# Down product of a hybrid decoder layer: smaller raw tiles, loads one buffer sooner, and a new order on VectorE

## The chip, the cores and the metric

The kernel runs on one core of one Trainium2 chip. The metric is the time of one execution in microseconds (us) of device time. Five engines work side by side, each through its own list of instructions in order: TensorE (PE in the profile; its weight loads are PEld), VectorE (DVE), ScalarE (ACT), GpSimd (POOL) and SyncE (SP), which here only issues DMAs. An instruction waits for semaphores, and what stands behind it on its engine waits with it.

## The reference, cut to what matters

One layer with 512 tokens and a width of 1024: input projections, retention and sparse attention, an output projection with a layer norm, then a SwiGLU feed-forward net of 2816 hidden units and a second layer norm. The change touches the feed-forward net alone:

```python
gate, up = jnp.split(x @ w_gate_up, 2, axis=-1)
ffn = (jax.nn.silu(gate) * up) @ w_down
return layer_norm(DEEPNORM_ALPHA * x + ffn, ln_ffn_gain, ln_ffn_bias)
```

## The kernel before, in words

**Precision.** Every product of two f32 matrices is made of three matmuls in the format fp32r (`mm3`): high part times high part, high times low, low times high. `split` (L84) makes the parts of a tensor: ACT casts it to the high part (L86). The low part is the source minus the high part, either on DVE (L91), or (where its engine argument is `None`) by a scaled copy on ACT (L88), which writes the negated source, and a DMA with addition that POOL issues (L89). The second matmul of an `mm3` needs the low part of the weights, the first only the high one.

**Gate stage.** 22 tiles of hidden units, one `g_cycle` each, seven groups of 12 matmuls a cycle. The weights come as raw tiles `graw`, DVE forms sums of them (`g_sum`, L815, four instructions), and `g_conv` splits the kinds A, B, C, D. Cycle 2 splits kind C of tile 3, whose low part is `gl3C`.

**Down product.** 11 pairs of hidden tiles, `hu`. Five pairs (`PLAIN`: 0, 1, 2, 3 and 10) are multiplied plainly, column half by column half: first the left half, into four PSUM banks (`d_mm`, `l_step`). The other six pairs form three units (2, 3, 4) and are multiplied in Strassen-like blocks: seven products q, in the order 1, 5, 6, 2, 7, 4, 3, for each unit j. This makes 21 blocks (`w_mm(0)` to `w_mm(20)`), each of 12 matmuls. Block i uses the weights that `w_prep` has split, called p{q}_{j} below: blocks 0 to 2 use p1_2, p1_3, p1_4; 3 to 5 p5_2 to p5_4; 6 to 8 p6; 9 to 11 p2; 12 to 14 p7; 15 to 17 p4; 18 to 20 p3. The split of block i+4 is issued behind block i, since its four buffers for each part (tags `wh`, `wl`) are those of the block that has just been read. Left operands are split by `aprep` into tiles called slot, often with a low part by DMA.

**Raw weights.** All raw weight tiles, `graw` and those of the down product, share three buffers (tag `raw`, 8 KB in each partition), and a new load takes the buffer that was set free first. In order: `draw` 0 and 1 (pairs 0 to 3), `draw` 2 (pair 10 alone, which fills half of a buffer), `r1_2`, `r1_3`, `r1_4` (for p1), `r2a`, `r2b`, `r3a`, `r4_2`, `r4_3`, `r4_4` (for p7), `r5a`, `r5b`, then the right half of the plain pairs. All of them are issued by SP, in this order. `r2a` comes into the buffer of `r1_2`, `r2b` into that of `r1_3`, `r3a` into that of `r1_4`; `r4_3` takes that of `r3a`, which is free after p2_3, and `r4_4` that of `r2b`, free after p2_4.

**Sums on DVE.** `t1_` (L1155) subtracts parts of `r1` into small tiles `tw`; `t2_` (L1165) subtracts `tw` from `r2a` and `r2b` in place; `t4_` (L1169) makes `tw` anew from `r3a`, `r2b` and `r2a`; `t3_` (L1173) works in place on `r4`. `s1_` to `s4_` add and subtract blocks of the hidden tiles. `take` (L1212) and `add_to` (L1215) add finished PSUM banks to the result. The banks X hold products 1, 6 and 7, the banks Y product 5. The small tiles have 12 buffers (tag `t`).

Of the kernel before, what the change touches and what calls it, by code (L numbers as in the profile page):

```python
# [16 lines left out]
S = 512  # L17
# [36 lines left out]
def hybrid_layer_kernel(ctx: ExitStack, tc: tile.TileContext, xT, x, pos, w0, wf, wt, wo,  # L54
# [18 lines left out]
    def tmp(name, dt=F32):  # L73
        return tp.tile([P, 512], dt, tag="t", name=name)
# [732 lines left out]
    def g_sum(n, eng=V, which=slice(0, 4)):  # L807
        if n >= NF:
            return
        g, u = graw[n][:, 0], graw[n][:, 1]  # L810
        if n not in gsum:
            gsum[n] = [tmp(f"gs{n}_{i}") for i in range(4)]
        t = gsum[n]
        for dst, a, b in ((0, u[:, :S], g[:, :S]), (1, u[:, S:], t[0]), (2, u[:, S:], u[:, :S]), (3, g[:, S:], t[1]))[which]:
            eng.tensor_tensor(t[dst], a, b, op=ALU.subtract)  # L815
# [58 lines left out]
    def g_cycle(n, between=None):  # L874
        nxt = n + 1 if FIRST <= n + 1 < NF else None
        g_mm(n, "a", "A", 0, "s2", False)
        if n and not held(n - 1):
            g_end(n - 1)
        if between:
            next(between)  # L880
        gp[n]["c"] = psu(f"gc{n}")[:, :Q]
        g_mm(n, "c", "A", 1, "s1", True)
        t = tmp(f"gt{n}")
        gp[n]["t2"], gp[n]["t7"] = t[:, :Q], t[:, Q:]
        A.copy(gp[n]["t2"], gp[n]["a"])
        if n == 1:
            for m in range(FIRST):
                g_silu1(m)
        if n not in (1, 2):
            g_conv(n + 1, "A")  # L890
        if nxt:
            g_open(nxt)
            g_mm(nxt, "a", "B", 0, "11", True)
        g_mm(n, "a", "C", 0, "s3", False)
        if nxt:
            g_t1(nxt)
            g_mm(nxt, "b", "B", 1, "12", True)
        if held(n - 1):
            g_mm(n - 1, "c", "D", 0, "s4", False)
        if n == 0:  # L900
            g_mm(3, "b", "B", 1, "12", True)
        c = gp[n]["c"]
        if n == NF - 1:
            c = tmp("gc")[:, :Q]
            A.copy(c, gp[n]["c"])
            g_mm(n, "c", "D", 0, "s4", False)
        A.copy(gp[n]["t7"], gp[n]["a"])
        if n == 0:
            for b in (2, 3):
                combine("s4", b)  # L910
                hi("s4", b)
            g_sum(1, V, slice(2, 4))
        if n == 1:
            g_conv(2, "A")
            g_sum(2, V, slice(2, 4))
        V.tensor_tensor(gp[n]["t7"], gp[n]["t7"], c, op=ALU.add)
        if n == 2:
            g_conv(3, "A")
        if between:
            next(between)  # L920
        if n == 2:
            g_end(n - 1)
        if n + 2 >= FIRST:
            g_conv(n + 2, "B")
        if n == 0:
            g_add1(3)
        g_mm(n, "a", "C", 1, "22", False)
        if nxt:
            g_u1(nxt)
        if n > 1:  # L930
            g_sum(n + 2)
        g_conv(n + 1, "C")
        if n == 1:
            g_end(0)
            g_sum(3)
        if n == 0:
            for b in (2, 3):
                lo("s4", b)
            g_sum(2, V, slice(0, 2))
        if n < NF - 1 and not held(n):  # L940
            g_mm(n, "c", "D", 0, "s4", False)
        A.activation(gp[n]["h2"], gp[n]["a"], AF.Silu)
        g_conv(n + 1, "D", V if n else None)
        g_load(n + 4)
# [110 lines left out]
    UNITS = [2, 3, 4]  # L1055
# [11 lines left out]
    def wprep(key, pieces, low=V):  # L1067
        wh = wp.tile([P, 1024], F32R, tag="wh", bufs=4, name=f"dh{key}")
        wl = wp.tile([P, 1024], F32R, tag="wl", bufs=4, name=f"dl{key}")
        n = 1024 // len(pieces)  # L1070
        for i, src in enumerate(pieces):
            hi, lo = (t[:, i * n:i * n + n] for t in (wh, wl))
            if len(src.shape) == 3:
                hi, lo = (t.rearrange("p (k c) -> p k c", c=S) for t in (hi, lo))
            split(low, hi, lo, src)
        dw[key] = wh, wl
# [2 lines left out]

    def d_load(c, g):  # L1080

        pairs = ((0, 1), (2, 3), (10,))[g]
        draw[c, g] = raw_load(f"draw{c}_{g}", [(2 * i, wd[k, :, :, c * S:c * S + S]) for i, k in enumerate(pairs)])

    def conv_w(c, k):
        if k == 10:
            t, i = draw[c, 2] if c == 0 else r5b, 0 if c == 0 else 2
        else:
            t, i = draw[c, k // 2], 2 * (k % 2)
        wprep((c, k), [t[:, i:i + 2].rearrange("p k c -> p (k c)")])  # L1090

    def conv_h(m):
        j = m // 2
# [29 lines left out]
    def pq(t):  # L1123
        return t.rearrange("p (q c) -> p q c", q=2)
# [53 lines left out]
    def odd(t, k):  # L1178
        return t.rearrange("p (q k) c -> p q k c", k=2)[:, :, k]

    prep = {
        1: lambda j: wprep(f"p1_{j}", [odd(r1[j], 0)], None),
        5: lambda j: wprep(f"p5_{j}", [tw[j, 0], tw[j, 1]]),
        6: lambda j: wprep(f"p6_{j}", [flat(b22(j))]),
        2: lambda j: wprep(f"p2_{j}", [flat(b21(j))]),
# [6 lines left out]
    def w_prep(i):  # L1192
        q, j = WORDER[i]
        prep[q](j)
# [52 lines left out]
    g_cycle(NF - 2)  # L1247
    d_load(0, 1)
    g_cycle(NF - 1, prepare_down())
    d_load(0, 2)  # L1250
    g_end(NF - 1)

    def r1_load(j):
        r1[j] = raw_load(f"r1_{j}", [(2 * q, wd[2 * j + q, :, 0]) for q in range(2)])
# [4 lines left out]
    A.activation(idle, idle, AF.Sqrt)  # L1259
    left = [psu(f"dl{b}") for b in range(NB)]  # L1260
    r1_load(2)
    conv_w(0, 2)
    conv_h(2)
    for b in range(3):
        for i in range(2):
            d_mm(left[b], 0, i, b, i == 0, False)
    conv_w(0, 3)
    r1_load(3)
    conv_h(3)
    for i in range(2):  # L1270
        d_mm(left[3], 0, i, 3, i == 0, False)
# [4 lines left out]
    conv_h(10)  # L1276
    t1_(2)
    conv_w(0, 10)
    r1_load(4)
    w_prep(0)  # L1280
    r2a = raw_load("r2a", [(i, wd[4 + i, :, 1, S:]) for i in range(4)])

# [5 lines left out]
    t1_(3)  # L1288
    for j in UNITS:
        aprep(5, j, pq(ts[j]), V)  # L1290
    w_prep(1)
    r2b = raw_load("r2b", [(i, wd[8 + i, :, 1, S:]) for i in range(2)] + [(2 + i, wd[8 + i, :, 1, :S]) for i in range(2)])
    t1_(4)

    l_step(3)
    for j in UNITS:
        s2_(j)
    for j in UNITS:
        aprep(6, j, pq(ts[j]), V)
    t2_(2)  # L1300
    w_prep(2)
    r3a = raw_load("r3a", [(i, wd[4 + i, :, 1, :S]) for i in range(4)])
    t2_(3)
    t2_(4)
# [10 lines left out]
    for i in range(18):  # L1315
        q, j = WORDER[i]
        w_mm(i, home_of[q], q in (1, 5))
        if i == 0:
            for u in UNITS:
                s4_(u)  # L1320
        elif i == 1:
            t4_(2)
            t4_(3)
        elif i == 2:
            for t in range(2):
                take(t, cl, X[t])
        elif i == 3:
            aprep(2, 2, blk(2, 0, 1), None)
            aprep(2, 3, blk(3, 0, 1), None)
        elif i == 4:  # L1330
            aprep(2, 4, blk(4, 0, 1), None)
        elif i == 6:
            t4_(4)
        elif i == 7:
            aprep(7, 2, pq(t3s[2]), None)
            t3_(2)
        elif i == 8:
            for u in (3, 4):
                aprep(7, u, pq(t3s[u]), None)
        elif i == 9:  # L1340
            t3_(3)
        elif i == 10:
            t3_(4)
            for u in UNITS:
                aprep(4, u, blk(u, 1, 1), None)
            gf = big.tile([P, 2, D], F32, tag="s8", name="gbf")
            for k, v in enumerate((lfg, lfb)):
                dma(gf[:, k], row(v, D))
        elif i == 12:
            for u in UNITS:  # L1350
                aprep(3, u, pq(ts[u]), None)
        if i < 17:
            w_prep(i + 4)
        else:
            conv_w(1, 10)
        if i == 3:
            r4_load(2)
        elif i == 7:
            r4_load(3)
            r4_load(4)  # L1360
        elif i == 8:
            r5a = raw_load("r5a", [(n, wd[4 + n, :, 1, S:]) for n in range(4)])
        elif i == 9:
            r5b = raw_load("r5b", [(n, wd[8 + n, :, 1, S:]) for n in range(2)] + [(2, wd[10, :, :, S:])])
        elif i == 10:
            d_load(1, 0)
        elif i == 15:
            d_load(1, 1)
        if i == 5:
            for t in range(2):  # L1370
                take(t, cr, Y[t])
            for t in range(2):
                take(2 + t, cr, Y[t])
        elif i == 8:
            for t in range(2):
                add_to(t, cr, X[t])
        elif i == 14:
            for t in range(2):
                take(2 + t, cl, X[t])
            for t in range(2):  # L1380
                add_to(2 + t, cr, X[t])
        elif i == 16:
            for b in range(2):
                add_to(b, cl, left[b])
                stat(b, 0, cl)
        elif i == 17:
            for b in range(2, NB):
                add_to(b, cl, left[b])
                stat(b, 0, cl)
# [106 lines left out]
```

## Time and profile before

| what | value |
|---|---|
| median of 3 runs | 625.13 us (624.58 to 625.94) |
| the profiled execution, its own time | 625.04 us |
| its span from the first to the last instruction | 623.2 us |
| PE busy | 609.9 us, 98% |
| DVE busy | 511.5 us, 82% |
| ACT busy | 325.2 us, 52% |
| POOL busy | 115.7 us, 19% |
| mean granted TensorE clock | 0.997 of full speed |

The profiled execution stands for the others: its time is 0.09 us from the median. The 1.8 us between its span and its time lie around the instructions. The gate stage runs in the middle of the span up to about 499.8 us, the down product behind it. Times in the rows are us from the first instruction. A row of a timeline gives the start, the duration, the engine, the line, the operation, what is written and read, and the count; in brackets stand the idle time before it and what ended it. A row for several instructions in a row gives their duration together.

### The profile page before, as it was taken

How to read it: one execution, taken by the hardware profiler on the slowest of the kernel's cores; microseconds unless marked ns; L12 is line 12 of the kernel's file. 1: busy time of each engine (PE TensorE's matmuls, PEld its weight loads, DVE VectorE, ACT ScalarE, POOL GpSimd, SP SyncE). 2: the span in 40 equal slices, each digit the busy share in tenths (PEclk: the TensorE clock that was granted, in tenths of full speed). 3: DMA queues.
4: the chain of work that ended last, by engine and by line, in shares of the span. 5: the costliest groups of instructions: out<-in, count | busy, mean ns of one | idle time of the engine just before them, and what ended most of it. 6: DMA issues, size and time to landing. Idle time of an engine off the chain costs nothing.

```text
span 623.2 us, 9845 instructions
## 1 busy us (share of the span) xinstructions
PE 609.9 (98%) x3732; PEld 544.4 (87%) x3732; DVE 511.5 (82%) x950; ACT 325.2 (52%) x577; POOL 115.7 (19%) x119
## 2 busy tenths in 40 slices
PE   9999999999999999999999999999999999899995
PEld 7888888888888778889999999999999988687884
DVE  6798687897879877989998888889898896886956
ACT  5643444334333765877645555555465694548300
POOL 1177332421455000241000000000000021214011
PEclk9999999999999999999999999999999999999998
DMA  8877444788544862695433323231413269689602
GB/s 310 282 227 198 137 116 121 199 179 196 135 102 105 327 262 85 160 223 108 127 105 124 103 103 131 73 136 69 136 69 135 102 159 264 160 198 307 212 35 101
DMA packets 31840, 98.49 MB, mean 158 GB/s; under 512 B 3328, under 2 KB 9024, under 8 KB 26160
## 3 DMA queue, kind: packets, MB, share of 16 engines
q1 hardware_dynamic: 20448, 76.23, 35.5%
q0 software_dynamic: 10608, 20.39, 17.9%
q10 hardware_dynamic: 736, 1.25, 0.6%
q8 instruction: 29, 0.48, 0.3%
q14 instruction: 19, 0.16, 0.1%
HBM read 74.52 MB, written 2.10 MB: 123 GB/s over the span
## 4 chain that ended last, share of the span: by engine, by line
PE 70%; DVE 15%; DMA 6%; ACT 3%; issue 3%; POOL 1%; SPq 0%; POOLq 0%; ACTq 0%; DVEq 0%
PE ga L846 17%; PE gc L846 9%; PE pf L96 5%; PE pf L95 5%; PE pf L94 5%; PE gb L846 4%; DMA r<-in_wd_dram 3%; PE pt L94 3%; PE pt L96 3%; PE pt L95 3%; DVE gs L815 2%; PE mx L96 2%; PE mx L94 2%; PE mx L95 2%; PE dr L94 2%
## 5 line engine op out<-in xcount | busy, mean ns | idle before, releaser
L86 ACT CAST wh<-raw 128x1024 fp32r<-128x1024 f32 x44 | 45.9, 1049 | 44.3 <-issue 18.4
L89 POOL DMA_DIRECT2D slot<-hu x9 | 10.9, 1317 | 230.1 <-ACT slot L88 229.5
L96 PE MATMUL pf<-xh,wl 128*128 128x512 f32 x128 | 50.0, 391 | 0.3 <-DVE wl L91 0.3
L94 PE MATMUL pf<-xh,wh 128*128 128x512 f32 x128 | 50.1, 391 | 0.0
L95 PE MATMUL pf<-xl,wh 128*128 128x512 f32 x128 | 50.0, 391 | 0.0
L91 DVE TENSOR_TENSOR wl<-raw,wh 128x1024 fp32r<-128x1024 f32 x25 | 30.5, 1231 | 16.9 <-ACT wh L86 16.6
L94 PE MATMUL pt<-wh,xh 128*128 128x512 f32 x96 | 39.2, 408 | 0.0
L96 PE MATMUL pt<-wh,xl 128*128 128x512 f32 x96 | 37.6, 392 | 0.0
L95 PE MATMUL pt<-wl,xh 128*128 128x512 f32 x96 | 37.5, 390 | 0.0
L435 POOL TENSOR_TENSOR rs<-ve,half 128x1 f32<-128x1 f32 (+1 forms) x11 | 11.8, 1069 | 103.9 <-DVE ve L434 97.8
L815 DVE TENSOR_TENSOR gs<-graw,gs 128x512 f32<-128x512 f32 x44 | 30.3, 688 | 0.8
L815 DVE TENSOR_TENSOR gs<-graw 128x512 f32<-128x512 f32 x44 | 30.1, 685 | 0.0
L96 PEld LDWEIGHTS pf<-xh,wl 128*128 128x128 f32 x128 | 24.0, 188 | 5.8 <-DVE wl L91 0.7
L95 PEld LDWEIGHTS pf<-xl,wh 128*128 128x128 f32 x128 | 24.1, 188 | 4.6
L94 PEld LDWEIGHTS pf<-xh,wh 128*128 128x128 f32 x128 | 24.1, 188 | 4.6
L397 DVE MAX8 m<-score 128x8 f32<-128x256 f32 (+2 forms) x48 | 26.8, 558 | 1.1
L89 POOL DMA_DIRECT2D wl<-raw x19 | 16.9, 890 | 57.1 <-ACT wl L88 50.3
L398 DVE MATCH_REPLACE8 score<-m,score 128x256 f32<-128x256 f32 (+2 forms) x48 | 26.0, 542 | 0.0
L380 ACT ACTIVATE lg<-lg 128x256 f32<-128x256 f32 (+2 forms) x24 | 10.9, 474 | 24.6 <-PE lg L379 22.4
L96 PEld LDWEIGHTS pt<-wh,xl 128*128 128x128 f32 x96 | 18.0, 188 | 3.9
L95 PEld LDWEIGHTS pt<-wl,xh 128*128 128x128 f32 x96 | 18.1, 189 | 3.1
L94 PEld LDWEIGHTS pt<-wh,xh 128*128 128x128 f32 x96 | 18.1, 189 | 3.1
(1121 smaller groups left out, 2082.5 us busy)
## 6 DMA issues: line engine op xcount, KB each, us to landing
graw<-in_wgu_dram SPq DMA_DIRECT2D x22, 1024.0 KB, 4.8
wl<-raw POOLq DMA_DIRECT2D x19, 512.0 KB, 5.5
raw<-in_wf_dram SPq DMA_DIRECT2D x8, 1024.0 KB, 6.4
raw<-in_wo_dram SPq DMA_DIRECT2D x8, 1024.0 KB, 4.9
raw<-in_wt_dram SPq DMA_DIRECT2D x6, 1024.0 KB, 5.2
r<-in_wd_dram SPq DMA_DIRECT2D x12, 512.0 KB, 5.9
draw<-in_wd_dram SPq DMA_DIRECT2D x9, 512.0 KB, 5.3
w0s<-in_w_dram SPq DMA_DIRECT2D x8, 320.0 KB, 5.1
```

Source lines behind the costliest of these rows:

```text
L86: A.copy(hi, src)
L89: nc.gpsimd.dma_start(lo.bitcast(F32), src, accum_op=ALU.add)
L91: eng_lo.tensor_tensor(lo, src, hi.bitcast(F32), op=ALU.subtract)
L94: T.matmul(acc, lhsT=lh, rhs=rh, start=first, stop=False, **kw)
L95: T.matmul(acc, lhsT=lh, rhs=rl, start=False, stop=False, **kw)
L96: T.matmul(acc, lhsT=ll, rhs=rh, start=False, stop=last, **kw)
L380: A.activation(lp[:, :n], lp[:, :n], AF.Relu)
L397: V.max(m8, a)
L398: V.match_replace(out=a, in_to_replace=m8, in_values=a, imm_value=TAKEN)
L435: G.tensor_tensor(r[:, :n], e[:, :n], half[:, :n], op=ALU.pow)
L815: eng.tensor_tensor(t[dst], a, b, op=ALU.subtract)
L846: T.matmul(gp[n][acc], lhsT=a[:, i * S + k * P:i * S + k * P + P], rhs=parts[q][:, b, k], start=first and j == 0, stop=j == 11, skip_group ...
```

## The change

- Raw weights of pair 10, left half: no longer a half-filled tile of tag `raw`, but two tiles `d10` of tag `t`, loaded by two DMAs on SP between the loads of `r1_2` and `r1_3`; their split is done in two pieces. So `r1_2`, `r1_3`, `r1_4` each come into the buffer that was one place earlier in the row of loads, and their loads stand earlier in the program.
- p1_4: the low part is made on DVE instead of by DMA with addition.
- `t1_(4)` stands ahead of p1_3 and of the load of `r2b`. p1_4 stands behind the first two of the three splits of product 6's left operand and ahead of `t2_(2)`.
- The four additions out of the banks Y stand two behind block 7 and two behind block 9, instead of all behind block 5. `t3_(2)` stands behind block 8 instead of block 7.
- Gate stage, cycle 2: the sums of tile 4 are formed behind the split of kind C of tile 3, not ahead of it.

```diff
-        if n > 1:
+        if n > 2:
             g_sum(n + 2)
         g_conv(n + 1, "C")
         if n == 1:
             g_end(0)
-            g_sum(3)
+        if n in (1, 2):
+            g_sum(n + 2)
...
-        pairs = ((0, 1), (2, 3), (10,))[g]
+        pairs = ((0, 1), (2, 3))[g]
...
-        if k == 10:
-            t, i = draw[c, 2] if c == 0 else r5b, 0 if c == 0 else 2
+        if k == 10 and c == 0:
+            wprep((c, k), d10)
         else:
-            t, i = draw[c, k // 2], 2 * (k % 2)
-        wprep((c, k), [t[:, i:i + 2].rearrange("p k c -> p (k c)")])
+            t, i = (r5b, 2) if k == 10 else (draw[c, k // 2], 2 * (k % 2))
+            wprep((c, k), [t[:, i:i + 2].rearrange("p k c -> p (k c)")])
...
-        1: lambda j: wprep(f"p1_{j}", [odd(r1[j], 0)], None),
+        1: lambda j: wprep(f"p1_{j}", [odd(r1[j], 0)], None if j < 4 else V),
...
-    d_load(0, 2)
     g_end(NF - 1)
...
     r1_load(2)
+    d10 = [tmp(f"d10_{i}") for i in range(2)]
+    for i in range(2):
+        dma(d10[i], wd[10, :, i, :S])
+    r1_load(3)
     conv_w(0, 2)
...
     conv_w(0, 3)
-    r1_load(3)
+    r1_load(4)
...
     conv_w(0, 10)
-    r1_load(4)
     w_prep(0)
...
+    t1_(4)
     w_prep(1)
     r2b = raw_load("r2b", [(i, wd[8 + i, :, 1, S:]) for i in range(2)] + [(2 + i, wd[8 + i, :, 1, :S]) for i in range(2)])
-    t1_(4)
...
-    for j in UNITS:
+    for j in UNITS[:2]:
         aprep(6, j, pq(ts[j]), V)
+    w_prep(2)
+    aprep(6, 4, pq(ts[4]), V)
     t2_(2)
-    w_prep(2)
...
         elif i == 7:
             aprep(7, 2, pq(t3s[2]), None)
+        elif i == 8:
             t3_(2)
-        elif i == 8:
...
-        if i == 5:
+        if i == 7:
             for t in range(2):
                 take(t, cr, Y[t])
+        elif i == 9:
             for t in range(2):
                 take(2 + t, cr, Y[t])
```

## Rows read from the trace of the kernel before

**Rows 1.** Who waited for whom, PE alone, over the whole span: engine, tile and line, what it waited for, then us in total, times, the longest.

```profile
PE dx L95 <- DMA dlp<-r: 2.9, 1, 2.9
...
PE dx L95 <- DVE dlp L91: 0.6, 1, 0.6
PE ga L846 <- DVE gl3C L91: 0.5, 1, 0.5
```

**Rows 2.** The chain of waits, in order of time, at a place in the gate stage where nothing waits: start, duration, and one group of 12 matmuls.

```profile
391.96 1.44 PE ga L846 x12
```

**Rows 3.** The timeline of PE, single matmuls: in cycle 3 of the gate stage the first two matmuls of kind C of tile 3 and the first of the next group; in the down product the first matmul of block 0, of block 2 with its second and the first of block 3, and of block 14 with its second and the first of block 15.

```profile
314.72 0.28 PE L846 MATMUL ga<-parts,gh3C 128*128 128x256 f32 x1
315.50 0.38 PE L846 MATMUL ga<-parts,gl3C 128*128 128x256 f32 x1 [0.50 <-DVE gl3C L91]
...
316.91 0.28 PE L846 MATMUL gb<-part,gh4B 128*128 128x256 f32 x1
...
527.02 0.39 PE L94 MATMUL dx<-dhp,slot 128*128 128x512 f32 x1
...
532.46 0.39 PE L94 MATMUL dx<-dhp,slot 128*128 128x512 f32 x1
535.74 0.50 PE L95 MATMUL dx<-dlp,slot 128*128 128x512 f32 x1 [2.89 <-DMA dlp<-r]
...
538.37 0.39 PE L94 MATMUL dy<-dhp,slot 128*128 128x512 f32 x1
...
568.29 0.39 PE L94 MATMUL dx<-dhp,slot 128*128 128x512 f32 x1
569.29 0.50 PE L95 MATMUL dx<-dlp,slot 128*128 128x512 f32 x1 [0.62 <-DVE dlp L91]
...
571.93 0.39 PE L94 MATMUL dl<-dhp,slot 128*128 128x512 f32 x1
```

**Rows 4.** The timeline of DVE in cycles 2 and 3 of the gate stage: the low parts of kind B of tile 4, of kind C of tile 3 and, a cycle on, of kind C of tile 4.

```profile
311.02 1.29 DVE L91 TENSOR_TENSOR gl4B<-graw,gh4B 128x512 fp32r<-128x512 f32 x2
...
314.76 1.29 DVE L91 TENSOR_TENSOR gl3C<-gs,gh3C 128x512 fp32r<-128x512 f32 x2
...
323.32 1.28 DVE L91 TENSOR_TENSOR gl4C<-gs,gh4C 128x512 fp32r<-128x512 f32 x2
```

**Rows 5.** The timeline of SP, which issues the loads: r1_2, r1_3, r1_4, r2a, r2b, then r4_3 and r4_4.

```profile
499.72 0.81 SPq L80 DMA_DIRECT2D r<-in_wd_dram  x2
...
506.39 0.80 SPq L80 DMA_DIRECT2D r<-in_wd_dram  x2
...
513.38 1.02 SPq L80 DMA_DIRECT2D r<-in_wd_dram  x2
...
523.51 1.75 SPq L80 DMA_DIRECT2D r2a<-in_wd_dram  x4
...
526.13 1.75 SPq L80 DMA_DIRECT2D r2b<-in_wd_dram  x4
...
554.38 1.19 SPq L80 DMA_DIRECT2D r<-in_wd_dram  x2
...
556.65 1.48 SPq L80 DMA_DIRECT2D r<-in_wd_dram  x2
```

**Rows 6.** The timeline of POOL: its issues of the DMAs with addition that make the low parts of p1_2, p1_3 and p1_4.

```profile
513.20 1.19 POOL L89 DMA_DIRECT2D dlp<-r  x1 [2.54 <-ACT dlp L88]
518.69 1.19 POOL L89 DMA_DIRECT2D dlp<-r  x1 [4.29 <-ACT dlp L88]
527.95 1.19 POOL L89 DMA_DIRECT2D dlp<-r  x1 [8.08 <-ACT dlp L88]
```

**Rows 7.** Who waited for whom, SP alone, between 520 and 537 us, when it issues r2a, r2b and r3a: what they waited for, us in total, times, the longest.

```profile
SPq L80 <- DMA dlp<-r: 17.5, 3, 9.0
```

**Rows 8.** The DMA queues: of POOL (q0) between 519 and 524 us, and of SP (q1) between 526 and 531 us: packets, MB, share of the 16 engines' time.

```profile
q0 software_dynamic: 412, 0.80, 87.2%
...
q1 hardware_dynamic: 791, 1.43, 91.9%
```

**Rows 9.** The timeline of DVE in the down product: the second instruction of t1_(4); t2_(4); the low part of p5_2; those of p6_2 and p6_3; the four additions out of the banks Y; t3_(3), the low part of p7_3, and t3_(4).

```profile
522.54 0.69 DVE L1155 TENSOR_TENSOR tw<-r 128x512 f32<-128x512 f32 x1 [2.03 <-DMA r<-in_wd_dram]
...
529.99 1.29 DVE L1165 TENSOR_TENSOR r2b<-r2b,tw 128x512 f32<-128x512 f32 x2 [0.64 <-DMA r2b<-in_wd_dram]
...
533.01 1.28 DVE L91 TENSOR_TENSOR dlp<-tw,dhp 128x512 fp32r<-128x512 f32 x2
...
545.00 2.36 DVE L91 TENSOR_TENSOR dlp<-r2a,dhp 128x1024 fp32r<-128x1024 f32 x2
...
549.54 2.48 DVE L1212 SCALAR_TENSOR_TENSOR x<-x,dy 128x512 f32<-128x512 f32 x4
...
561.46 1.23 DVE L1173 TENSOR_TENSOR r<-r 128x1024 f32<-128x1024 f32 x1 [2.31 <-DMA r<-in_wd_dram]
563.93 1.23 DVE L91 TENSOR_TENSOR dlp<-r,dhp 128x1024 fp32r<-128x1024 f32 x1 [1.24 <-ACT dhp L86]
565.55 1.23 DVE L1173 TENSOR_TENSOR r<-r 128x1024 f32<-128x1024 f32 x1 [0.40 <-DMA r<-in_wd_dram]
```

**Rows 10.** The timeline of ACT in the down product: the high part of p5_3, which waits for block 0, and the high part of p7_3, which waits for t3_(3).

```profile
529.99 1.14 ACT L86 CAST dhp<-tw 128x512 fp32r<-128x512 f32 x2 [1.30 <-PE dx L96]
...
562.84 1.05 ACT L86 CAST dhp<-r 128x1024 fp32r<-128x1024 f32 x1 [6.14 <-DVE r L1173]
```

## The prediction

> **What bounds the kernel now.** I read the page first: PE is busy for 98% of the span, so little but PE's own waits can be won. Then who waited for whom, PE alone, over the whole span: three waits matter, 2.9, 0.6 and 0.5 us [rows 1]. Then the timeline of PE at these places, since a wait costs more than its idle time: the matmuls behind it also run late. A group of 12 takes 1.44 us in the gate stage [rows 2]; the one of tile 3, kind C, takes 316.91 - 314.72 = 2.19, so 0.75 is lost. A block of the down product takes (532.46 - 527.02) / 2 = 2.72; block 2 takes 538.37 - 532.46 = 5.91 and loses 3.19; block 14 takes 571.93 - 568.29 = 3.64 and loses 0.92 [rows 3]. That is 4.86 us in all, 0.8% of the time. Last I read the timelines of the engines that feed these places. Behind the last block PE goes on without a wait, and the chain from its last matmul to the end stays as it is; what PE gains there, the time gains.
>
> **Gate tile 3.** PE is held by the first half of gl3C, which DVE starts at 314.76, behind four sums of tile 4 [rows 4]. The change puts the sums behind it. The low part of kind B of tile 4 starts at 311.02 and lasts 1.29, so gl3C's first half is there at 312.31 + 0.7 = 313.0, and PE's second matmul wants it at 314.72 + 1.44/12 = 314.84. Gain: 0.75. The four sums end 1.2 us later; next to be late would be gl4C: its first half is there at 323.32 + 0.68 = 324.0 [rows 4], and PE, by then 0.75 earlier, wants it seven groups later, at 314.84 + 7 x 1.44 = 324.9. So moving the sums costs nothing. All times below are in the frame of the old trace, without this 0.75.
>
> **Loads and p1_4.** Block 2 waits for the DMA with addition of p1_4 [rows 1, 3]. It was issued at 527.95 [rows 6], because p1_4 stood behind t1_(4), which waited for r1_4 until 522.54 [rows 9]; r1_4's load was issued only at 513.38, when pair 10 had left its buffer [rows 5]. Now r1_2 comes into the buffer that pair 10 had, r1_3 is issued where r1_2 was (499.72) and r1_4 where r1_3 was (506.39) [rows 5]. With the 9.2 us that r1_4 takes now (513.38 to 522.54, at the longest) it lands by 515.6. The high part of p1_4 then waits for its buffer, which is free when l_step(3) has run. This ends one step of 24 matmuls, 5.44 us, ahead of 527.02, at 521.6; a cast begins 0.25 after the next group's first matmul (529.99 against block 1's start at 529.74) [rows 3, 10], so at 521.8. The low part follows 1.09 later (562.84 to 563.93) and lasts 1.23 [rows 9, 10]: ready at 524.2, wanted at 532.69. Gain: 3.19, with 8 us to spare. What else these instructions cost: DVE gets one low part more and ACT loses a scaled copy, both while DVE would wait for r1_4 or r2b. Behind DVE's new wait stand a split of product 6 (wanted at block 8) and t2_(2), which waits for r2a anyway. POOL loses an issue. On SP two DMAs replace one and stand ahead of r1_3; SP has nothing else to do there until 499.7. The small tiles come from a pool of 12, whose oldest are gate sums read long before. If a tile of the last gate cycle had to be waited for (some 502 us), r1_3 would land 2.3 later and still in time. The second piece of pair 10's split costs ACT and DVE under 0.1 us each. All this I cost at nothing.
>
> **What is late next: r2b.** r2a, r2b and r3a wait for the additions of p1_2, p1_3 and p1_4 to land [rows 7]. r3a now only needs p1_4's DVE instruction and goes out right behind r2b, at 526.13 + 1.75 = 527.9 instead of past 535.74 [rows 3, 5]. At the 0.311 MB/us that SP's queue moved here (1.43 MB in 5 us at 92%) [rows 8] the 2.1 MB of both take 6.7 us, some 534, and t4_ wants r3a at 537.2. r2b still waits for p1_3's addition, issued by POOL at 518.69, which now lands by 526.1, 7.4 us on [rows 5, 6]. If that stays, t2_(4) starts at 529.99 and p5_2's low part at 533.01 as today [rows 9]. From there DVE runs without a gap, 0.60 for each instruction on 512 columns and 1.14 for 1024 (2.48 for four and 2.36 for two, less the overlap) [rows 9]: p5_2, three of s4_, p5_3, four of t4_, p5_4 and two additions make 15 x 0.60 = 9.0, so p6_2's low part is ready at 542.0 + 1.2 = 543.2. Block 6 wants it with its second matmul, at 527.02 + 6 x 2.72 + 2.72/12 = 543.57. Blocks 3 to 5 have 0.5 to 1.7 to spare, so the margin is 0.3 at block 6: I cost it at nothing. How long p1_3's addition takes now is not shown. Nearest rows: its own 7.4 us, 7.8 for p1_4's (527.95 to 535.74) and 10.3 for p1_2's (513.20 to 523.51, when r2a goes out) [rows 3, 5, 6]. Up to 7.7 it costs nothing, and less gains nothing, since no block waits for it; at 10.3 r2b is 2.9 late and block 6 waits 2.6. I take its own.
>
> **What is late after that: block 14.** Its wait in the old trace ends a chain through r4_4: load issued at 556.65, t3_(4) at 565.55 [rows 5, 9]. Both loads now go out earlier, as the four additions no longer stand ahead of p2_3 and p2_4 on DVE. p2_3's cast follows block 6 (546.31), so r4_3 goes out at 546.31 + 1.09 + 1.22 = 548.6; p2_4's follows block 7 (549.03), so r4_4 goes out at 551.3. With today's time from issue to t3_ (7.1 and 8.9) [rows 5, 9] they are there at 555.7 and 560.2. But the two pairs of additions now stand in this very chain. On DVE, one after another: p2_4's low part starts at 549.03 + 1.09 = 550.12; + 1.14 and the additions of Y + 1.20 gives t3_(2) at 552.46. A t3_ and its low part take 1.38 to the cast (561.46 to 562.84), 1.09 to the low part and 1.14: 3.61 [rows 9, 10]. So the additions out of X start at 556.07, t3_(3) at 557.27, the second additions of Y at 560.88, t3_(4) at 562.08. Both loads are in time by 1.5 us or more. p7_4's low part is ready at 562.08 + 1.38 + 1.09 + 1.22 = 565.77, and block 14 wants it at 527.02 + 14 x 2.72 + 0.23 = 565.33. So a wait of 0.44 stays, between a bound of 0 and, were the loads late, more (below), and with the 0.15 by which the rest of such a block is late (571.93 - 569.29 for 11 matmuls, against 2.49) the block loses 0.59. Gain: 0.92 - 0.59 = 0.33. Blocks 12 and 13 want p7_2 and p7_3 at 559.89 and 562.61 and get them at 556.1 and 561.0. What follows (p4, p3, the right half) is tied to these blocks and moves with them.
>
> **The sum.** 0.75 + 3.19 + 0.33 = 4.27. Against the profiled execution's 625.04 that gives 620.8; the median of the runs stands 0.09 higher, so 620.9.
>
> **The rivals.**
> - **No wait is left in block 14.** All 4.86 are won: 620.3. For it: 0.44 us is little at the end of a chain of 16 us. Against it: each term is a measured row, and DVE can't pull anything forward, as it takes its list in order.
> - **r2b comes late.** p1_2's addition took 10.3 us with r1_4's 1.05 MB beside it, 3.4 us of work at 0.311 MB/us; without that, r2a goes out at some 520. So r2a travels beside p1_3's addition, whose 0.52 MB need 2.9 us (0.80 MB in 5 us at 87% is 0.183 MB/us) [rows 8]. If both end together, 6.3 us behind the end of POOL's issue at 519.9, the last byte is there at 526.2, before it is reported. I price that at 1.0 later than now: block 6 waits 0.7 and is 0.15 slower, 621.7. Against it: r1_4's 1.05 MB leave this same stretch. At the bound of 10.3 it is 623.6.
>   The Trainium skill (DMA: Bandwidth & Descriptors, Queues, rings and completion order) says that each DMA engine takes turns between its queues packet by packet. The trace agrees that they share: POOL's queue took 87% of the engines' time in a stretch in which SP's r1_4 was still landing [rows 8, 9]. By that rule this rival, 621.7, would be the forecast.
> - **The loads don't move.** If r1_2 got no earlier buffer, r1_4 would still land at 522.5. Then p1_4's cast and low part on DVE would follow t1_(4) and the splits, done by some 528, still ahead of 532.69: some 621.
> - **Slower: r4_3 late.** Its load now starts beside the DMAs with addition of product 7. t3_(3) wants it at 557.27, 8.7 us after its issue; each us beyond delays p7_3 and, DVE being in order, p7_4 and block 14 by one. At 13 us the whole gain is spent, from 14.2 the kernel is slower by over 0.2%, say 627. For it: two more waiting instructions behind each t3_ than now. Against it: 7.1 us at most today [rows 5, 9].
>
> **How the numbers follow.** A measurement of this kernel tells 0.2%, 1.25 us, from no change. Chances: forecast 0.56, no wait in block 14 0.12, r2b late 0.17 (0.03 of it within 0.2%), loads don't move 0.05, r4_3 late 0.10 (0.04 within, 0.06 slower). So faster 0.87, same 0.07, slower 0.06. The range runs from 619.8, the best case less the 0.55 by which the lowest run lies below the median, to 623.6, r2b at its bound; it leaves out r4_3 late and little else.
>
> **What would show it.** In the new profile: no wait at gl3C; none for a DMA in block 2; r1_4 issued near 505.6 and r3a right behind r2b; in block 14 a wait of about 0.4 for DVE, with t3_(4) started straight behind the additions and not by a DMA. A wait in blocks 3 to 6 would make the r2b step wrong; t3_(3) or t3_(4) released by a DMA, the r4 step.

## The result, and the profile after

The changed kernel takes 620.76 us in the median of four runs (620.34 to 621.16), against 625.54 of the kernel before (624.58 to 626.98) beside it: ratio 0.9922, 95% interval 0.9900 to 0.9943. Forecast were 620.9 and a range of 619.8 to 623.6. The profiled execution is the slowest of the four, 621.16 us with a span of 619.4; it lies 3.88 below the one before, where the sum had 4.27.

Who waited for whom, PE alone, the changed kernel, the two of its five rows that lie in the feed-forward net:

```profile
PE dx L95 <- DVE dlp L91: 0.2, 1, 0.2
PE gc L846 <- DVE gt L916: 0.2, 1, 0.2
```

The wait for the DMA of p1_4 and that for gl3C [rows 1] are gone. The wait of block 14 is down from 0.6 to 0.2. One is new: the last group of cycle 3 of the gate stage (`gc`) waits for an addition on DVE (L916). The other three rows (1.2, 0.4 and 0.2 us) belong to stages ahead of the gate.

The timeline of PE, the changed kernel: kind C of tile 3, the waiting group, and the first matmul of tile 4's kind A; blocks 0, 2 (two matmuls) and 3; block 14 with its second matmul, block 15, and block 18:

```profile
314.33 0.28 PE L846 MATMUL ga<-parts,gh3C 128*128 128x256 f32 x1
...
318.97 0.38 PE L846 MATMUL gc<-parts,gh3D 128*128 128x256 f32 x1 [0.16 <-DVE gt L916]
...
320.50 0.28 PE L846 MATMUL ga<-parts,gh4A 128*128 128x256 f32 x1
...
526.28 0.39 PE L94 MATMUL dx<-dhp,slot 128*128 128x512 f32 x1
...
531.72 0.39 PE L94 MATMUL dx<-dhp,slot 128*128 128x512 f32 x1
531.95 0.39 PE L95 MATMUL dx<-dlp,slot 128*128 128x512 f32 x1
...
534.44 0.39 PE L94 MATMUL dy<-dhp,slot 128*128 128x512 f32 x1
...
564.36 0.39 PE L94 MATMUL dx<-dhp,slot 128*128 128x512 f32 x1
564.99 0.50 PE L95 MATMUL dx<-dlp,slot 128*128 128x512 f32 x1 [0.23 <-DVE dlp L91]
...
567.62 0.39 PE L94 MATMUL dl<-dhp,slot 128*128 128x512 f32 x1
...
575.78 0.39 PE L94 MATMUL dr<-dhp,slot 128*128 128x512 f32 x1
```

Against [rows 3]: block 2 takes 534.44 - 531.72 = 2.72, the undisturbed time, where it took 5.91. Block 14 takes 567.62 - 564.36 = 3.26, where it took 3.64; its second matmul starts 0.40 late. Blocks 0 to 17 take 575.78 - 526.28 = 49.50.

The kernel before, two matmuls that stand in no group: the first of tile 4's kind A and the first of block 18.

```profile
321.23 0.28 PE L846 MATMUL ga<-parts,gh4A 128*128 128x256 f32 x1
...
580.09 0.39 PE L94 MATMUL dr<-dhp,slot 128*128 128x512 f32 x1
```

So blocks 0 to 17 took 580.09 - 527.02 = 53.07 [rows 3]: 3.57 are won there. The four gate groups from kind C of tile 3 to tile 4 took 321.23 - 314.72 = 6.51 and now take 320.50 - 314.33 = 6.17: 0.34. Undisturbed they are 4 x 1.44 = 5.76.

The timeline of SP, the changed kernel: r1_2, r1_3, r1_4, r2a, r2b, r3a, r4_3, r4_4:

```profile
492.62 0.81 SPq L80 DMA_DIRECT2D r<-in_wd_dram  x2
...
498.98 0.81 SPq L80 DMA_DIRECT2D r<-in_wd_dram  x2
...
505.65 0.81 SPq L80 DMA_DIRECT2D r<-in_wd_dram  x2
...
519.74 2.83 SPq L80 DMA_DIRECT2D r2a<-in_wd_dram  x4
...
524.02 1.75 SPq L80 DMA_DIRECT2D r2b<-in_wd_dram  x4
525.88 1.79 SPq L80 DMA_DIRECT2D r3a<-in_wd_dram  x4
...
547.87 1.20 SPq L80 DMA_DIRECT2D r<-in_wd_dram  x2
550.58 1.40 SPq L80 DMA_DIRECT2D r<-in_wd_dram  x2
```

Each load of r1 stands one place earlier than in [rows 5], r3a goes out right behind r2b, and r4_3 and r4_4 go out 6.5 and 6.1 us sooner. r2b too goes out sooner, by 2.1, of which 0.74 is the earlier start of the down product.

Three stretches of PE tell the parts of the change apart better than whole runs do: **gate**, from the first matmul of kind C of tile 3 to that of kind A of tile 4; **blocks**, from the first of block 0 to the first of block 18; **end**, from the first matmul into the last bank (`dc`) to the end of the span. What lies between them is the same in every kernel here (205.8 and 32.8 us). What lies ahead of the gate is not: kind C of tile 3 starts between 313.5 and 315.6 us, in kernels that don't differ up to there. All from the profiled executions; the medians are of whole runs, with that of the kernel before measured beside them:

| kernel | median | before | gate | blocks | end |
|---|---|---|---|---|---|
| before | 625.54 | | 6.51 | 53.07 | 10.3 |
| changed | 620.76 | 625.54 | 6.17 | 49.50 | 10.8 |
| e1 gate order alone | 625.50 | 624.71 | 6.17 | 53.54 | 10.4 |
| e2 changed, p1_4 by DMA | 622.04 | 624.71 | 6.16 | 50.41 | 10.8 |
| e3 changed, loads as before | 621.37 | 624.71 | 6.16 | 50.27 | 10.4 |
| e4 both of these undone | 625.13 | 624.71 | 6.18 | 53.72 | 10.4 |
| e5 additions as before | 622.71 | 626.49 | 6.16 | 50.94 | 10.8 |
| e6 second additions later | 620.55 | 626.49 | 6.18 | 48.96 | 10.8 |
| e7 changed, one DMA less | 620.58 | 626.49 | 6.17 | 49.50 | 10.3 |
| e8 before, one DMA more | 626.48 | 626.49 | 6.51 | 56.79 | 10.7 |
| e0 changed again | 620.83 | 627.00 | 6.16 | 49.48 | 10.8 |
| e9 three edits | 620.20 | 627.00 | 5.76 | 49.12 | 10.4 |
| e10 changed, third time | 621.01 | 627.38 | 6.17 | 49.50 | 10.8 |
| e11 three edits again | 619.97 | 627.38 | 5.76 | 49.20 | 10.3 |

The changed kernel repeats its stretches to 0.02; the kernel before spreads from 622.16 to 629.76 in 61 runs, the changed one from 620.34 to 621.78 in 14. The spread goes with TensorE's granted clock. Among the 59 runs of the kernel before that were measured beside the experiments, the 32 with a mean clock of 0.994 of full speed or less took 624.78 to 629.76, the 13 with 0.997 or more 622.16 to 625.65; the 14 of the changed kernel lie at 0.996 to 0.998. Where the clock falls is shown under e4.

### The profile page after: what moved, and what is told of

It is laid out like the page before. It is cut to its first block, busy times and chain, and to the rows that moved or that the text cites. A ratio compares the mean times of both kernels' runs of the same rounds, so it can differ in the third digit from the quotient of the medians.

```text
span 619.4 us, 9844 instructions
## 1 busy us (share of the span) xinstructions
PE 609.4 (98%) x3732; PEld 544.7 (88%) x3732; DVE 512.3 (83%) x952; ACT 324.4 (52%) x577; POOL 114.1 (18%) x118
## 4 chain that ended last, share of the span: by engine, by line
PE 73%; DVE 15%; ACT 4%; issue 4%; POOL 1%; DMA 1%; ACTq 0%; POOLq 0%; DVEq 0%
PE ga L846 17%; PE gc L846 9%; PE pf L96 5%; PE pf L95 5%; PE pf L94 5%; PE gb L846 4%; PE dl L95 2%; PE dl L94 2%; PE dl L96 2%; PE pt L94 2%; PE pt L96 2%; PE pt L95 2%; DVE gs L815 2%; PE dr L96 2%; PE dr L95 2%
```

## The experiments

**e1: the gate order alone.** The first hunk of the diff, on the kernel before.

> The kernel before with nothing but the new order in cycle 2 of the gate stage. By the prediction's step the second matmul of kind C of tile 3 finds gl3C ready, PE has no wait there, the group takes 1.44 us instead of 2.19, and block 0 of the down product starts 0.75 earlier, at 526.3: 0.75 us less than before, ratio 0.9988. Rival: the sums, now 1.2 us later, make kind C of tile 4 late, and the wait moves there: no change.

Whole runs don't settle it: ratio 0.9997, interval 0.9978 to 1.0016. The stretch does: 6.17, so 0.34 is won, neither 0.75 nor nothing. Its timeline of DVE in cycle 3, low part of kind A of tile 4 and the addition behind it:

```profile
316.99 1.29 DVE L91 TENSOR_TENSOR gl4A<-gs,gh4A 128x512 fp32r<-128x512 f32 x2
318.19 0.41 DVE L916 TENSOR_TENSOR gt<-gt,gc 128x256 f32<-128x256 f32 x1
```

L916 reads the bank `gc`, into which the last group of the cycle goes on adding. It ends at 318.60, and PE starts that group at 318.66. Undisturbed, three groups behind kind C, it would be 314.03 + 3 x 1.44 = 318.35. The wait moved there, not to tile 4's kind C.

**e2: p1_4's low part by DMA, all else as changed.**

```diff
-        1: lambda j: wprep(f"p1_{j}", [odd(r1[j], 0)], None if j < 4 else V),
+        1: lambda j: wprep(f"p1_{j}", [odd(r1[j], 0)], None),
```

> The changed kernel, but the low part of p1_4 is again made by the DMA with addition. Theory: the earlier loads alone carry the step. The cast follows l_step(3) at some 521, POOL issues at some 523.5, and with the 6 to 7.8 us that such additions took it lands at 529.5 to 531.3, ahead of 532.0 when block 2 wants it: no wait in block 2, time as the changed kernel, 620.8. Rival: DVE's low part is what counts: block 2 waits 1 us or more for the DMA, or r3a, which then waits for the addition, makes block 5 wait: 621.8 or more.

622.04. The theory held for block 2, which doesn't wait, and failed for the time. Block 5 waits; DVE and PE show why (second subtraction from r2b; second matmul of block 5):

```profile
530.80 0.69 DVE L1166 TENSOR_TENSOR r2b<-r2b,tw 128x512 f32<-128x512 f32 x1 [2.71 <-DMA r2b<-in_wd_dram]
```

```profile
540.58 0.50 PE L95 MATMUL dy<-dlp,slot 128*128 128x512 f32 x1 [0.35 <-DVE dlp L91]
```

The addition of p1_4 now runs beside r2b's load. In the changed kernel the same two instructions follow each other and wait for nothing, the second at some 527.9:

```profile
527.33 1.29 DVE L1166 TENSOR_TENSOR r2b<-r2b,tw 128x512 f32<-128x512 f32 x2
```

So the second is 2.9 us later in e2. The rival was right that DVE's low part counts, but through r2b, not through block 2 or r3a.

**e3: the loads as before, p1_4's low part on DVE.** `draw` 2 again a raw tile, `d10` gone, each `r1_load` at its old place.

> The changed kernel with the loads as before (pair 10 in a raw tile), the low part of p1_4 still on DVE. Theory, as the prediction's rival of loads that don't move: r1_4 lands at some 521.8, p1_4 is ready at some 527, 5 us ahead of block 2, and the margin at block 6 goes to 0 to 0.3: 620.5 to 621.2. Rival: the loads are what counts, and what stands behind p1_4 on DVE (t2_, p5_2, p5_4) comes late for blocks 3 to 6: 622 to 623.

621.37, 0.17 above the theory's band. Block 2 doesn't wait. Block 5 does, again behind r2b:

```profile
530.26 1.29 DVE L1166 TENSOR_TENSOR r2b<-r2b,tw 128x512 f32<-128x512 f32 x2 [0.48 <-DMA r2b<-in_wd_dram]
```

```profile
540.64 0.50 PE L95 MATMUL dy<-dlp,slot 128*128 128x512 f32 x1 [0.28 <-DVE dlp L91]
```

**e4: both undone.** e3 with e2's edit.

> The changed kernel with the loads as before and the low part of p1_4 by the DMA with addition, so without both halves of that step. Theory: the wait in block 2 comes back, 2.0 to 2.9 us long, since the addition is issued at 526.6 to 527.2 and takes 7 to 7.8: 623 to 623.9. Rival: the order of the splits alone (p1_4 ahead of one split of product 6) brings it in time: below 621.5.

The wait in block 2 is back (PE, block 2's second matmul):

```profile
535.73 0.50 PE L95 MATMUL dx<-dlp,slot 128*128 128x512 f32 x1 [2.31 <-DMA dlp<-r]
```

It is 0.58 shorter than before, and block 14 loses 0.37 less, and yet the blocks take 53.72, 0.65 more than before. The 1.6 between are the clock. PE behind this wait, the kernel before, then e4, then e8, which stands further down (the stretch; its length, busy time and matmuls; the granted clock as a share of full speed; share of the DMA engines, GB/s):

```profile
537.00:540.00 3.00, 3.00 (x15) 1.00 0.93 322
```

```profile
537.00:540.00 3.00, 3.00 (x8) 0.50 0.94 315
```

```profile
536.00:539.00 3.00, 3.00 (x8) 0.50 0.80 270
```

In e4 and e8 the granted clock fell behind the wait to 0.50, the lower of its two levels (1.2 GHz), and then rose again. Some eight matmuls stand 0.43 apart instead of 0.23, so 1.6 us go there. In the profiles of the kernel before and of e1, waits of 2.89 and 2.40 us left the clock at 1.00; e4's was 2.31, e8's 2.92. So the length of the wait alone does not decide it, and what does is not shown. In no other profile here does the clock fall in the blocks.

The median, 625.13, lies 1.2 above what was expected, and the expectation had no term for the clock. That this is the cause is likely, not shown: the profiled execution is the slowest of twelve (626.25), and the others have no trace. With e2 and e3: either half takes the wait out of block 2 (3.3 and 3.5 us of blocks, some 1.6 of them the clock in e4's profile), and only both keep r2b clear (0.9 and 0.8 more).

**e5: the additions and `t3_(2)` back at their places.**

> The changed kernel with the four additions out of the banks Y behind block 5 and t3_(2) behind block 7, as before. Theory: moving them only exchanged one limit for another. r4_3 goes out some 2 us later and r4_4 1.5 us later than in the changed kernel, t3_(4) starts at 560.6 to 562 (561.25 there) and is again released by the DMA of r4_4; block 14 waits 0 to 1.1 us: 620.3 to 621.7, the same within what can be told. Rival: the additions set when the loads start, and all of their 2.4 us come back at block 14: 622.5 or more.

622.71: as the rival said in size. The profiled execution is the second fastest of seven (621.74), and its timeline shows the theory's mechanism, and one more. DVE, t3_(3) and t3_(4); then PE, blocks 14 and 15:

```profile
557.09 1.23 DVE L1174 TENSOR_TENSOR r<-r 128x1024 f32<-128x1024 f32 x1 [3.15 <-DMA r<-in_wd_dram]
...
561.13 1.23 DVE L1174 TENSOR_TENSOR r<-r 128x1024 f32<-128x1024 f32 x1 [0.35 <-DMA r<-in_wd_dram]
```

```profile
564.90 0.50 PE L95 MATMUL dx<-dlp,slot 128*128 128x512 f32 x1 [0.76 <-DVE dlp L91]
...
568.54 0.50 PE L96 MATMUL dl<-dhp,slot 128*128 128x512 f32 x1 [0.40 <-DMA slot<-hu]
```

Both t3_ wait for their loads again, and block 15 waits for the addition of product 4's left operand. So moving the additions and `t3_(2)` is worth 1.44 us of the blocks in this profile (50.94 - 49.50), though it leaves a wait of its own. What the slower runs lose beyond that is in no trace, and the two moves were not tried one by one.

**e6: the second pair of additions behind block 11.**

```diff
-        elif i == 9:
+        elif i == 11:
             for t in range(2):
                 take(2 + t, cr, Y[t])
```

> The changed kernel with its second pair of additions out of Y behind block 11 instead of block 9. Theory: the wait left in block 14 is DVE's list, in order, in which this pair stands. Without it t3_(4) starts when r4_4 lands, near 560.4, 0.8 earlier, and p7_4 is ready at 564.1, ahead of 564.6: no wait in block 14, and 0.5 us less, 620.2. Rival: the load of r4_4 or ACT's list of casts sets it: block 14 still waits, 620.8.

Block 14 doesn't wait, and blocks 0 to 17 take 18 x 2.72 = 48.96: 0.54 won, as expected. DVE's t3_(4) is now released by the load, as predicted:

```profile
559.79 1.23 DVE L1174 TENSOR_TENSOR r<-r 128x1024 f32<-128x1024 f32 x1 [0.16 <-DMA r<-in_wd_dram]
```

The median of whole runs is 0.28 under that of the changed kernel (e0), which was measured apart from it.

**e7 and e8: the end of the kernel.** In the changed kernel SP issues one DMA more. e7 takes one away far from it; e8 gives one to the kernel before.

```diff
-            r5b = raw_load("r5b", [(n, wd[8 + n, :, 1, S:]) for n in range(2)] + [(2, wd[10, :, :, S:])])
+            r5b = raw_load("r5b", [(0, wd[8:10, :, 1, S:].rearrange("k p c -> p k c")), (2, wd[10, :, :, S:])])
...
+        if g == 2:
+            pieces = [(i, wd[10, :, i, c * S:c * S + S]) for i in range(2)]
```

> The changed kernel with the first two pieces of r5b in one DMA instead of two, so as many DMAs on SP as before the change. Theory: the time from the last matmul to the end depends on how many DMAs SP issues, as the closing waits on their semaphores run in a fixed order, and what stands behind the wait for the last landing adds 0.06 each. The stretch from the first dc matmul to the end shrinks from 10.8 to 10.37, as in the kernel before: 0.43 less, 620.3. Rival: the last DMA itself took longer in that profile: 10.8 again.

> The kernel before with the load of pair 10 in two DMAs of half the size, into the same raw tile, so one DMA more on SP. By the theory of the closing waits the stretch from the first dc matmul to the end grows from 10.37 to 10.8, and nothing else changes: 0.43 more than before, 625.1 against a median of 624.7 in many runs. Rival: the stretch stays at 10.4.

The stretch follows the number: 619.5 - 609.18 = 10.3 in e7, 626.8 - 616.06 = 10.7 in e8. All fourteen profiles agree: 10.3 to 10.4 with the old number of DMAs on SP, 10.7 to 10.8 with one more. Whole runs can't tell 0.4 us (e8: ratio 0.9999, 0.9974 to 1.0023). SP's closing instructions on semaphores, the changed kernel, up to the landing of the last DMA at 618.0 and behind it (count; shortest, median and longest in ns; first and last start):

```profile
L1497 SPq EVENT_SEMAPHORE  x3: 17/28/28, 616.2 to 618.0; - x3
...
L1497 SPq EVENT_SEMAPHORE  x8: 28/28/28, 618.0 to 618.5; - x8
```

The kernel before, up to the landing at 622.3, and the next of SP behind it:

```profile
L1492 SPq EVENT_SEMAPHORE  x10: 17/28/28, 620.5 to 622.3; - x10
...
L1492 SPq DRAIN  x1: 13/13/13, 622.4 to 622.4; - x1
```

Before, the wait for the last landing was the last of ten, and the others were done while the DMA flew. Now it is the third (counted in both rows), and seven of some 0.06 us each stand behind it. The number of DMAs decides this; which DMA uses which semaphore is not shown.

**e0, e9, e10 and e11: the changed kernel again, and a version with three edits.** e6, e7's edit, and in the gate stage:

```diff
         V.tensor_tensor(gp[n]["t7"], gp[n]["t7"], c, op=ALU.add)
+        if n == 3:
+            g_sum(4, V, slice(2, 4))
...
+        if n == 2:
+            g_sum(n + 2, V, slice(0, 2))
```

> The changed kernel once more, as the measure for the variants: 620.8, a wait of 0.2 in block 14, a stretch of 10.8 from the first dc matmul to the end, and four groups from kind C of tile 3 in 6.17.

> The changed kernel with three edits: the second pair of additions behind block 11, the first two pieces of r5b in one DMA, and, in the gate stage, the last two of the four sums of tile 4 only behind the addition of cycle 3 (L916) for which the last group of that cycle waits in the changed kernel. Theory: block 14 waits no more (0.5 less), the end is 0.43 shorter, and the four groups from kind C of tile 3 take 5.76 instead of 6.17 (0.41 less): 619.4 in all. Rival: DVE, which is full in those gate cycles, moves the wait to kind C of tile 4 or to tile 5, and only 0.9 is won: 619.9.

> The changed kernel a third time, beside the next kernel: 620.8, and the same three stretches as before (6.17 in the gate stage, 49.50 for blocks 0 to 17, 10.8 at the end).

> The kernel with the three edits once more, beside the changed kernel. The stretches promise 0.41, 0.38 to 0.54 and 0.43, 1.2 to 1.4 us less than the changed kernel: 619.5. Rival: the 0.6 us of the first comparison is all that arrives, 620.2, and a part is given back in the stretches ahead of the gate stage.

The gate takes its 5.76 and waits nowhere, the end 10.3 to 10.4, the blocks 49.12 and 49.20. Medians: 620.20 beside 620.83, and 619.97 beside 621.01, 0.6 and 1.0 of the 1.1 to 1.2 that the stretches promise. In the gate no wait moved on: L916 now runs 1.2 earlier, counted from kind C of tile 3. In the blocks 0.2 is left, since a next thing is late, block 15's third matmul, which reads the left operand's low part (e11, PE; no wait is put down to it, so that the low part held it, as in e5, is argued):

```profile
566.98 0.39 PE L95 MATMUL dl<-dlp,slot 128*128 128x512 f32 x1
567.33 0.50 PE L96 MATMUL dl<-dhp,slot 128*128 128x512 f32 x1
```

It starts 0.35 behind the one before, where 0.23 is usual. This version is the fastest of the study: 619.37 to 620.67 in nine runs.

## Why the prediction was right, point by point

**Block 2: right.** 3.19 were forecast and 3.19 came. Issues came as worked out: r1_4 at 505.65 (near 505.6), r3a right behind r2b. Its rival of loads that don't move, some 621, said that DVE's low part alone is enough for block 2; run as e3 it gave 621.37 and no wait there. What the prediction had not seen is that the earlier loads alone are enough too (e2); the wait returns in e4. It also had no term for the clock: 3.19 is what the wait costs in an execution that keeps its clock, and in e4 and e8 some 1.6 came on top.

**r2b: right that it is next, wrong that it stays.** The prediction left p1_3's addition at 7.4 us. It took 5.9, and r2b went out 1.4 us sooner in the frame of the down product. Lengths from issue to landing, the changed kernel, then e3, in which r1_4 still loads beside it:

```profile
dlp<-r POOLq DMA_DIRECT2D x1, 512.0 KB, 5.9
...
r2a<-in_wd_dram SPq DMA_DIRECT2D x4, 256.0 KB, 4.7
```

```profile
dlp<-r POOLq DMA_DIRECT2D x1, 512.0 KB, 7.0
```

So the margin at block 6 was larger than 0.3 in the changed kernel. The low parts of p6_2 and p6_3 (DVE):

```profile
539.37 2.36 DVE L91 TENSOR_TENSOR dlp<-r2a,dhp 128x1024 fp32r<-128x1024 f32 x2
```

The first is ready at some 540.6, and block 6 wants it at 526.28 + 6 x 2.72 + 0.23 = 542.83, 2.2 later. e2 and e3 show what this was for: with either half undone r2b is late and block 5 waits, not block 6, at which the prediction had put the least margin.

**r2b late: fell.** r2a did go out while p1_3's addition ran, at 519.74 (some 520 was forecast). The addition became shorter, not longer, and r2a's pieces took 4.7 us in the median, against 3.5 before:

```profile
r2a<-in_wd_dram SPq DMA_DIRECT2D x4, 256.0 KB, 3.5
```

The queues show what happened (packets, MB, the packets' time as a share of the 16 engines', which can pass 100%). The kernel before from 519 to 522 us, with r1_4 still loading; then the changed kernel from 519.7 to 522.2:

```profile
q0 software_dynamic: 204, 0.40, 72.4%
q1 hardware_dynamic: 123, 0.42, 38.1%
```

```profile
q0 software_dynamic: 211, 0.43, 110.7%
```

Before, the addition (q0) shared the engines with a load (q1). Now it had them alone: SP's queue moved nothing in this stretch, though r2a was issued at 519.74. Its first packets show between 522.8 and 523.0, some 3.1 us behind the issue; before, they show between 524.4 and 524.6, some 1 us behind it [rows 5]. By the Trainium skill's rule of turns between queues (DMA: Bandwidth & Descriptors, Queues, rings and completion order) the two would have shared. The changed kernel shows no turns here, while the kernel before shows both queues at work; whether r2a's packets already stood ready at the engines is not shown. So the rival failed at its condition: r2a did not travel beside the addition, and the load bore the delay.

**Block 14: right in kind and size.** Forecast: t3_(3) at 557.27, t3_(4) at 562.08, p7_4 ready at 565.77, so 556.53, 561.34 and 565.03 with the 0.74 of the earlier start. DVE, the changed kernel:

```profile
556.46 1.22 DVE L1174 TENSOR_TENSOR r<-r 128x1024 f32<-128x1024 f32 x1
558.91 1.23 DVE L91 TENSOR_TENSOR dlp<-r,dhp 128x1024 fp32r<-128x1024 f32 x1 [1.24 <-ACT dhp L86]
560.05 1.28 DVE L1213 SCALAR_TENSOR_TENSOR x<-x,dy 128x512 f32<-128x512 f32 x2
561.25 1.22 DVE L1174 TENSOR_TENSOR r<-r 128x1024 f32<-128x1024 f32 x1
563.71 1.23 DVE L91 TENSOR_TENSOR dlp<-r,dhp 128x1024 fp32r<-128x1024 f32 x1 [1.24 <-ACT dhp L86]
```

Neither t3_ waits for a DMA, the additions stand straight ahead of t3_(4), and p7_4 is ready at 564.94. The wait is 0.40 for 0.44, the loss 0.54 for 0.59. e6 confirms that the second pair of additions is its cause. The blocks together won 3.57, and 3.52 were forecast.

**Gate tile 3: the term was mis-sized.** The step that failed is "So moving the sums costs nothing": 0.75 was forecast, 0.34 came. The search for what is late next went to kind C of tile 4, seven groups on, and passed over L916, which stands on DVE behind gl4A. DVE and PE, the kernel before:

```profile
318.89 0.41 DVE L916 TENSOR_TENSOR gt<-gt,gc 128x256 f32<-128x256 f32 x1
```

```profile
319.79 0.28 PE L846 MATMUL gc<-parts,gh3D 128*128 128x256 f32 x1
```

L916 ended at 319.30, 0.49 ahead of the group that waits for it, and PE was to come 0.75 earlier. The new order left L916 where it was on DVE, 7.87 behind the start of gl4B (318.89 - 311.02, and 318.50 - 310.63 in the changed kernel), so PE met it. Putting two of the sums behind it (e9, e11) brings the other 0.41.

**"The chain from its last matmul to the end stays as it is": wrong by 0.4.** One DMA more on SP costs it (e7, e8). The prediction had counted that DMA on SP's queue, but not at the end.

**The sum.** Between the two profiled executions the blocks won 3.57 and the gate 0.34, and the stretches ahead of the gate were 0.39 shorter, which is no part of the change. That makes 4.30; the time fell by 3.88, so the end took back 0.42. The change itself is worth 3.57 + 0.34 - 0.42 = 3.49 here, where 4.27 was forecast: the missed terms, 0.41 and 0.42, are too much gain in the forecast, and 0.05 more came from the blocks. That the median fell on 620.76 all the same is in part luck. The forecast was made against one execution, 625.04, and all three profiles of the changed kernel reach the gate 0.36 to 0.70 earlier than that one did. Side by side the medians differ by more than forecast, 4.8, 6.2 and 6.4 us: the kernel before has medians from 624.71 to 627.38 in five series of runs, the changed one 620.76 to 621.01 in three, and many runs of the kernel before show a lower clock than the execution on which the forecast rests.

**Slower, r4_3 late: not in the changed kernel.** But e8's profile, the kernel before with one DMA more and 56.79 us in the blocks, shows such a chain where the old order stands: r4_3 goes out at 554.93, and t3_(3) waits for it until 563.90, 9.0 us on, against 7.1 in the profile of the kernel before; for 4.06 of them DVE does nothing else. Of e8's 3.72 us over the kernel before, some 1.6 are the clock. So what spreads the kernel before so widely is likely in part a clock that falls behind block 2's wait in some executions: e8 is all but the same kernel, and the mean clocks of the kernel's runs go with their times. What else spreads it, and why the clock falls only in some, was not settled. That the changed kernel, which has no wait in block 2, doesn't have this spread is shown by its runs.

## What to carry to other kernels

When instructions are moved on a full engine, look at every wait behind the place, the small ones first: the next to be late was a 256-column addition with 0.5 us to spare, not the large split seven groups on. A low part that a late load and a DMA with addition make late can be made on an engine, or its load moved forward; either took the first wait away here, and the second half paid at the next load. Behind a long wait of PE, read the granted clock as well: where it fell, the same wait cost some 1.6 us more. A closed stretch between two matmuls tells tenths of a microsecond where whole runs can't tell one.

## What was not expected of the hardware

- SP's closing waits cost some 0.4 us more or less by the number of DMAs it has issued: ten waits, of which those behind the last landing take some 0.06 us each.
- A DMA with addition of 512 KB took 7.0 us (e3) and 7.3 (the kernel before) beside a load that had started before it, and 5.9 where that load was gone. A load issued 1.8 us after it moved its first packet some 3.1 us behind its issue, and its pieces took 4.7 us to land in place of 3.5.
- Behind the wait in block 2 TensorE's granted clock fell to 0.50, its lower level of 1.2 GHz, in two profiles (waits of 2.31 and 2.92 us) and stayed at 1.00 in two others (2.40 and 2.89 us).
